# Seven-product gates: queries, keys and six gate columns in three rolling sets, the value pair gathered in PSUM banks, one weight sum made by adding transfers

## The chip, the cores and the metric

The kernel runs on one core of one Trainium2 chip. The metric is the device time of one execution in microseconds. Of the kernel before there are three timed runs and one profiled execution.

## The reference

One hybrid decoder layer on x (512 x 1024, float32): a pre-norm, one wide projection, three token mixers with gates, an output projection, a conv FFN and a final norm. The change lies in the projection and its first consumers.

```python
u = rmsnorm(x, ln1_g);  proj = u @ w_in            # 1024 -> 1152 q | 1152 k | 1152 v | 1024 pool |
                                                   #         1024 z | 1536 xbc | 16 dt | 3 x 1024 gates
q, k, v: 18 heads of 64 in 3 groups of 6 (dilations 1, 4, 16), each group banded causal attention
xbc = silu(causal_dwconv(xbc, conv_w, conv_b))     # 4 taps, 12 columns of 128
ga, gb, gc = sigmoid(gate_pre + b_gate)            # 8 columns of 128 each
m = ga * attn + gb * pool + gc * ssd;  x += m @ w_o;  x += conv_ffn(rmsnorm(x));  out = rmsnorm(x)
```

## The kernel before

**Matmuls in three terms.** float32 operands are split into a high part (float32r, cast on ScalarE) and a low part (the rest, subtracted on VectorE). A product is wh*xh + wh*xl + wl*xh, in this order (`mm3`, L234). A column of 128 outputs over 1024 inputs takes 24 matmuls of 512 columns.

**Jobs.** The work of TensorE is a list of `Job`s from `program()`. Each has weight sources, and before job n runs, a `prepare` step does three things for its successors: `low` (VectorE, L215) of the weights of job n+1, `cast` (ScalarE, L195) of those of n+2, and `fetch` (SyncE, L183) of those of n+3 into one of two `raw` tiles. The cast goes out in two halves through the list `second`: a half is emitted at each `step()`, or before the next job at the latest. A `job.form` gives a tile that is no fetched one, `job.then` is called behind the low part, and a `Call` runs a function at its place in the list.

**Steps.** `step()` first emits what is in `second`, then takes one more item from `waiting` (attention heads, scan chunks) and moves every running item on by one phase. An attention item (`attend`, L751 to L797) makes scores for two heads on TensorE, adds the bias and takes the maximum on VectorE, and makes four exponentials on ScalarE (L772); two steps later it turns them on TensorE.

**Queues.** The orders of TensorE, ScalarE, VectorE and GpSimd are the program's own. SyncE's transfers are ordered by the framework's scheduler.

**Quarter products.** For some products the 2 x 2 blocks of u and of the weights are multiplied in seven quarter products, with sums of u quarters (`sums_of_u`, `US`) and sums of weight quarters. Before, this is done for the value columns of groups 1 and 2 (`v_pair`, `sevens`: seven products into PSUM tiles `pb`, copied out and added on VectorE, L373 to L381 and L619) and for queries and keys of group 1 (`qk_sevens`: seven products of three columns, in banks). The eight gate columns of branch 1 are plain (`gate_jobs`, evacuated by a sigmoid and multiplied into the pool branch `MG`, L1166 to L1168), and so are the twelve columns of XBC (`xbc_evac`: one ScalarE pass, L911, and three convolution steps on VectorE, L915).

**Order of the stage:** pool branch; gates 0 to 3; the value pair; "one", "five", "two", "three" of queries/keys; gates 4 and 5; "six"; gates 6 and 7; "seven", "four"; `attend(1)`; XBC columns 0 to 11; the scan.

**Values.** The rows of the value columns are spread by sends from SBUF to SBUF, four for each 128 rows (`vr<-v`, L624), issued by SyncE.

Of the kernel before, what the change touches and what calls it, by code (L numbers as in the profile page):

```python
# [16 lines left out]
P = 128  # L17
# [66 lines left out]
def trunk(ctx: ExitStack, tc, out, x, rel_bias, ln1_g, w_in, b_gate, w_a, pool_w, pool_scale, w_b,  # L84
# [235 lines left out]
    def sums_of(f0, f1, ah, al, found):  # L320


        sa, sb = T("sa"), T("sb")
        dve.tensor_tensor(sa[:, LO], f0[:, HI], f1[:, HI], OP.add)
        dve.tensor_tensor(sa[:, HI], sa[:, LO], f0[:, LO], OP.subtract)
        dve.tensor_tensor(sb[:, LO], f0[:, LO], f0[:, HI], OP.subtract)
        dve.tensor_tensor(sb[:, HI], f1[:, LO], sa[:, HI], OP.subtract)
        yield
        bh, bl = T("sbh", F32R), T("sbl", F32R)
        act.copy(ah, sa)  # L330
        act.copy(bh, sb)
# [10 lines left out]
    def sevens(quarter, c, side, W, emit):  # L342

        r1, r2, r3, r5 = {}, {}, {}, {}

        def job(j, load, form, use):
            def body(ws):
                wh, wl = ws  # L350
                parts = side(j)
                for i in range(2):
                    ps = MM("pb")
                    o = slice(i * P, (i + 1) * P)
                    mm3(ps[:, :c], lambda k: wh[:, k, :], lambda k: wl[:, k, :],
                        lambda k: parts[k][0][:, o], lambda k: parts[k][1][:, o], range(4), flip=True)
                    use(i, ps[:, :c])
                step()
            new = Job([load] if load is not None else [], 4, c, body)
            new.form = form  # L360
            if load is None:
                new.load = lambda: None
            return new

        def keep(r, name):
            def use(i, ps):
                r[i] = T(name)[:, :c]
                act.copy(r[i], ps)
            return use

        def p5(i, ps):
            keep(r5, "r5")(i, ps)
            dve.tensor_tensor(r2[i], r2[i], ps, OP.add)  # L373

        def p6(i, ps):
            dve.tensor_tensor(r1[i], r1[i], ps, OP.add)
            emit(0, 1, i, r1[i], r2[i])

        def p7(i, ps):
            r3[i] = T("r3")[:, :c]  # L380
            dve.tensor_tensor(r3[i], r1[i], ps, OP.add)  # L381
            emit(1, 1, i, r3[i], r5[i])

        one = job("A11", quarter(0, 0), None, keep(r1, "r1"))
        two = job("A12", quarter(1, 0), None, lambda i, ps: emit(0, 0, i, r1[i], ps))
        three = job(4, None, lambda: W[1], keep(r2, "r2"))
        one.then = lambda: diff(one.raw, W[0], one.raw)
        three.then = lambda: diff(W[0], W[1], W[0])
        two.then = lambda: diff(W[1], W[1], one.raw)
        yield one  # L390
        yield three
        yield two
        yield job(1, None, lambda: one.raw, p5)
        yield job(2, None, lambda: W[1], p6)
        yield job(3, None, lambda: W[0], p7)
        yield job("A22", None, lambda: diff(two.raw, two.raw, W[1]),
                  lambda i, ps: emit(1, 0, i, r3[i], ps))
# [3 lines left out]
    def sums_of_u(p):  # L401

        f = []
        for k in (2 * p, 2 * p + 1):
# [4 lines left out]
                           lambda j, h, l: US.__setitem__((j, p), (h, l)))  # L409
# [195 lines left out]
    def v_pair():  # L605
# [3 lines left out]
        quarter = lambda two, h: rows_(c + 384 * h)[two]  # L609

        def load():
            for two in range(2):
                W.append(ypool.tile([P, 4, S], F32, name="w3", tag="xs")[:, :, :384])
                sp.dma_start(W[two], quarter(two, 1))

        def emit(hi, right, i, a, ps):
            g, tb = 1 + right, 2 * hi + i
            t = T(f"v{g}")
            dve.tensor_tensor(t[:, :384], a, ps, OP.add)  # L619

            for n in range(4):
                if (g, n) not in V:
                    V[g, n] = T(f"vr{g}")
                sp.dma_start(V[g, n][32 * tb:32 * tb + 32, :384], t[n:P:4, :384])  # L624

        return load, sevens(quarter, 384, side_u, W, emit)
# [20 lines left out]
    def qk_sevens(g):  # L647

        cols = (C_Q + 384 * g, C_K + 384 * g)
        q = lambda two, h: w_in[:, cols[h]:cols[h] + 384].rearrange(  # L650
            "(k two p) c -> two p k c", two=2, p=P)[two]
        W, X, Z, Y, r1, r5 = [], {}, {}, {}, {}, {}

        def load():
            for h in range(2):
                W.append(ypool.tile([P, 4, S], F32, name="w3", tag="xs")[:, :, :384])
                sp.dma_start(W[h], q(h, 1))

        def at(banks, c):
            return banks[c // 2][:, (c % 2) * 256:(c % 2) * 256 + 256]  # L660

        def half(which, c, hi):
            if (which, g, c) not in QK:
                QK[which, g, c] = T(f"{which}{g}")
            t = QK[which, g, c]
            t = grouped(t, g) if which == "q" else plain(t, g)
            return t[:, :, 64 * hi:64 * hi + 64]

        def turned_(ap):
            return ap.rearrange("p (j r) -> p r j", r=4)  # L670

        def job(source, j, banks, name, use, form=None):
            def body(ws):
                wh, wl = ws
                parts = side_u(j)
                for c in range(3):
                    fresh = name is not None
                    if fresh and c % 2 == 0:
                        banks[c // 2] = (MM if banks is Y else SM)(name)
                    cs = slice(c * P, (c + 1) * P)  # L680
                    mm3(at(banks, c), lambda k: wh[:, k, cs], lambda k: wl[:, k, cs],
                        lambda k: parts[k][0], lambda k: parts[k][1], range(4),
                        fresh and c % 2 == 0, True, again=not fresh or c % 2 == 1)
                    if c:
                        for done in (0, 1) if c == 1 else (2,):
                            use(done)
                        step()
            new = Job([source] if source is not None else [], 4, 384, body)
            new.form = form
            if source is None:  # L690
                new.load = lambda: None
            return new

        def keep(r, name, banks, scale):
            def use(c):
                r[c] = T(name)[:, :256]
                act.mul(r[c], at(banks, c), scale)
            return use

        def p2(c):  # L700
            dve.scalar_tensor_tensor(half("q", c, 0), turned_(at(Y, c)), 0.125, turned_(r1[c]),
                                     OP.mult, OP.add)

        def p6(c):
            r = T("r2")[:, :256]
            act.copy(r, at(X, c))
            dve.tensor_tensor(half("k", c, 0), turned_(at(Z, c)), turned_(r), OP.add)

        def p7(c):
            r = T("r7")[:, :256]  # L710
            act.copy(r, at(X, c))
            dve.tensor_tensor(half("k", c, 1), turned_(r), turned_(r5[c]), OP.add)

        def p4(c):
            act.mul(half("q", c, 1), turned_(at(X, c)), 0.125)

        one = job(q(0, 0), "A11", X, "p1", keep(r1, "r1", X, 0.125))
        one.then = lambda: diff(W[0], W[0], one.raw)
        two = job(q(1, 0), "A12", Y, "p2", p2)
        five = job(None, 1, Z, "p5", keep(r5, "r5", Z, 1.0), lambda: W[0])  # L720
        three = job(None, 4, Z, None, lambda c: None, lambda: W[1])
        three.then = lambda: diff(W[1], W[1], W[0])
        six = job(None, 2, X, None, p6, lambda: W[1])
        seven = job(q(0, 0), 3, X, None, p7, lambda: diff(seven.raw, W[1], seven.raw))
        four = job(q(1, 0), "A22", X, None, p4, lambda: diff(four.raw, four.raw, W[1]))
        return load, [one, five, two, three], [six, seven, four]

# [176 lines left out]
    def xbc_evac(m, ps):  # L904
        if m < 8:
            if m % 4 == 0:
# [253 lines left out]
    MG, MH, SG = {}, {}, {}  # L1160

# [314 lines left out]
    def program():  # L1476
# [11 lines left out]
        load, pair = v_pair()  # L1488
        yield Call(load)
# [266 lines left out]
```

## Time and profile before

| | us |
|---|---|
| timed runs | 1035.77, 1034.72, 1035.15; median 1035.15 |
| the profiled execution | 1034.7 |
| its span | 1033.0 |

| engine | busy us | share |
|---|---|---|
| TensorE (PE) | 1022.2 | 99% |
| weight loads (PEld) | 863.1 | 84% |
| VectorE (DVE) | 690.9 | 67% |
| ScalarE (ACT) | 473.3 | 46% |
| GpSimd (POOL) | 149.6 | 14% |

A row of the timeline or the chain begins with the start, counted in us from the span's start, and the length. A group of instructions names line, engine, operation, output and inputs, then shape and count; in brackets stand the idle time before it and what ended that. SPq is SyncE issuing transfers.

### The profile page before, as it was taken

Reading aid. Unit: us, or ns where it says so; the run is one execution under the profiler, and the core shown is the slowest. Engines: PE = TensorE matmul, PEld = TensorE weight load, DVE = VectorE, ACT = ScalarE, POOL = GpSimd, SP = SyncE. Lnnn points to the kernel's source line nnn. Section 1 sums busy time; section 2 is a strip of 40 time slices with the busy share of each in tenths; the row PEclk is TensorE's granted clock in tenths of the full one; section 3 lists DMA queues with packets and bytes.
Section 4 is the critical chain, followed back from the end, with each engine's and each line's share of the span. In section 5 each row is a group of like instructions: output and inputs, shape, how many; then the busy total and the mean of one; then the engine's idle time right before and its main releaser. Section 6 shows DMA issues by size and latency. Waiting matters only on the chain.

```text
span 1033.0 us, 13348 instructions
## 1 busy us (share of the span) xinstructions
PE 1022.2 (99%) x5312; PEld 863.1 (84%) x5312; DVE 690.9 (67%) x921; ACT 473.3 (46%) x779; POOL 149.6 (14%) x125
## 2 busy tenths in 40 slices
PE   9999999999999999999999999999999999999997
PEld 9998878899888878888888888898888888888885
DVE  5553566687567658766768656766768676666775
ACT  6432554453356364557445324545444443453342
POOL 2770000000000004210152501101111001111120
PEclk9999999999999999999999999999999999999999
DMA  8344312035242244452244525543233324323142
GB/s 289 115 129 138 109 54 75 31 102 172 94 139 84 86 127 116 144 140 67 67 148 152 174 82 204 171 141 121 82 102 124 102 82 163 123 81 122 62 143 82
DMA packets 115997, 122.35 MB, mean 118 GB/s; under 512 B 5315, under 2 KB 98310, under 8 KB 115935
## 3 DMA queue, kind: packets, MB, share of 16 engines
q1 hardware_dynamic: 115343, 120.64, 36.7%
q8 instruction: 42, 0.69, 0.3%
q10 hardware_dynamic: 592, 0.86, 0.3%
q14 instruction: 20, 0.16, 0.1%
HBM read 117.69 MB, written 2.22 MB: 116 GB/s over the span
## 4 chain that ended last, share of the span: by engine, by line
PE 93%; DVE 3%; ACT 2%; DMA 1%; issue 1%; ACTq 0%; SPq 0%; DVEq 0%
PE pa L234 35%; PE pu L234 21%; PE pb L234 10%; PE p L234 10%; PE pqk L234 6%; PE pa L1607 2%; PE ps L751 1%; PE pu L1407 1%; DVE wl L215 1%; PE ppw L234 1%; PE pt L779 1%; PE po L792 1%; PE py L1077 1%; ACT wh L195 1%; DMA xin<-in_x_dram 1%; PE pyo L1084 1%
## 5 line engine op out<-in xcount | busy, mean ns | idle before, releaser
L215 DVE TENSOR_TENSOR wl<-raw,wh 128x2048 fp32r<-128x2048 f32 (+3 forms) x96 | 218.5, 2278 | 46.7 <-ACT wh L195 38.8
L195 ACT CAST wh<-raw 128x1024 fp32r<-128x1024 f32 (+3 forms) x190 | 189.9, 1017 | 54.9 <-DVE raw L339 32.3
L1268 DVE SCALAR_TENSOR_TENSOR hc<-pu,fcol,hc 128x510 f32<-128x510 f32 x88 | 65.8, 748 | 61.0 <-ACT hc L1265 59.4
L234 PE MATMUL pa<-uh,wh 128*128 128x512 f32 x384 | 98.6, 399 | 0.0
L234 PE MATMUL pa<-ul,wh 128*128 128x512 f32 x384 | 94.9, 389 | 0.0
L234 PE MATMUL pa<-uh,wl 128*128 128x512 f32 x384 | 94.9, 389 | 0.0
L234 PEld LDWEIGHTS pa<-ul,wh 128*128 128x128 f32 x384 | 72.1, 188 | 15.2
L234 PEld LDWEIGHTS pa<-uh,wl 128*128 128x128 f32 x384 | 72.1, 188 | 14.9
L234 PE MATMUL pu<-uh,wl 128*128 128x512 f32 (+1 forms) x352 | 83.6, 380 | 0.2 <-DVE wl L215 0.2
L234 PE MATMUL pu<-uh,wh 128*128 128x512 f32 (+1 forms) x352 | 83.6, 379 | 0.0
L234 PE MATMUL pu<-ul,wh 128*128 128x512 f32 (+1 forms) x352 | 83.5, 379 | 0.0
L234 PEld LDWEIGHTS pa<-uh,wh 128*128 128x128 f32 x384 | 70.1, 188 | 14.5 <-issue 0.7
L234 PEld LDWEIGHTS pu<-uh,wl 128*128 128x128 f32 x352 | 64.1, 188 | 13.0 <-DVE wl L215 0.6
L234 PEld LDWEIGHTS pu<-ul,wh 128*128 128x128 f32 x352 | 64.2, 188 | 12.5
L234 PEld LDWEIGHTS pu<-uh,wh 128*128 128x128 f32 x352 | 64.1, 188 | 12.4
L1273 POOL TENSOR_TENSOR hc<-hc 128x512 f32<-128x512 f32 x22 | 30.4, 1383 | 279.2 <-DVE hc L1268 244.2
L1265 ACT ACTIVATE hc<-pu,fcol,fcol 128x512 f32<-128x512 f32 x40 | 31.2, 780 | 82.0 <-PE pu L234 81.7
L1039 POOL TENSOR_TENSOR xd<-xc,dec 128x512 f32<-128x512 f32 x6 | 6.4, 1063 | 331.5 <-DVE xc L1033 312.6
L772 ACT ACTIVATE sb<-sb,both 128x128 f32<-128x128 f32 (+1 forms) x72 | 30.1, 419 | 33.2 <-DVE both L769 23.2
L1166 ACT ACTIVATE sg<-pa,col 128x512 f32<-128x512 f32 x24 | 16.5, 688 | 58.1 <-PE pa L234 51.3
L1270 ACT ACTIVATE hc<-hc 128x512 f32<-128x512 f32 x22 | 13.9, 632 | 42.9 <-DVE hc L1268 42.9
L915 DVE SCALAR_TENSOR_TENSOR xs<-pa,col,xs 128x509 f32<-128x509 f32 (+2 forms) x24 | 18.0, 749 | 16.4 <-ACT xs L911 15.8
(377 smaller groups left out, 1863.1 us busy)
## 6 DMA issues: line engine op xcount, KB each, us to landing
raw<-in_w_in_dram SPq DMA_DIRECT2D x25, 1024.0 KB
raw<-in_ffn_w_up_dram SPq DMA_DIRECT2D x22, 1024.0 KB
raw<-in_ffn_w_down_dram SPq DMA_DIRECT2D x11, 1024.0 KB
raw<-in_w_o_dram SPq DMA_DIRECT2D x8, 1024.0 KB
raw<-in_w_in_dram SPq DMA_DIRECT2D x14, 512.0 KB
raw<-in_w_in_dram SPq DMA_DIRECT2D x8, 768.0 KB
raw<-in_w_b_dram SPq DMA_DIRECT2D x4, 1024.0 KB
al<-ad SPq DMA_DIRECT2D x16, 256.0 KB
```

The costliest lines, as they stand in the source:

```text
L195: act.copy(job.high[:, :, o], job.raw[:, :, o])
L215: (eng or dve).tensor_tensor(l[:, :, o], job.raw[:, :, o], h[:, :, o].bitcast(F32), OP.subtract)
L234: pe.matmul(ps, l, r, start=first and n == 0, stop=last and n == total - 1, skip_group_check=again)
L751: pe.matmul(pss[i][:, o:o + w * P], q[r, n * P:(n + 1) * P], k[r, kb * P:(kb + w) * P], start=True, stop=True)
L772: act.activation(sb[:, off:off + w * P], sb[:, off:off + w * P], AF.Exp, bias=nm[:, n, h:h + 1], accum_out=ls[:, n, h:h + 1])
L915: dve.scalar_tensor_tensor(t[:, sh:], ps[:, :S - sh], col[:, o_cw + 12 * k + m:o_cw + 12 * k + m + 1], t[:, sh:], OP.mult, OP.add)
L1166: act.activation(s, ps, AF.Sigmoid, bias=col[:, o:o + 1])
L1265: act.activation(t, ps, AF.Identity, bias=ff["c1"][:, ff["b"] + m:ff["b"] + m + 1], scale=fw(2, m))
L1268: dve.scalar_tensor_tensor(t[:, sh:], ps[:, :S - sh], fw(k, m), t[:, sh:], OP.mult, OP.add)
L1270: act.activation(t, t, AF.Silu)
L1273: pool.tensor_tensor(a, a, t, OP.mult)
L1607: pe.matmul(first[2 * n + j][:, lo:hi], a[:, k, j * P:(j + 1) * P], b[:, k, lo:hi], start=a is wh and b is uh and k == 0, stop=a is wl and ...
```

## The change

1. **Sets.** `qk_sevens` goes. `set_of_sevens` makes seven quarter products for two left and two right columns of 128 at a time, each product 24 matmuls of 256 columns into one bank. Three sets: queries 0, 1 with keys 0, 1; query 2 and gate 0 with key 2 and gate 1; gates 2, 3 with gates 4, 5. The sets roll: products of the next stand between those of the last. Four PSUM banks ("c", "y", "a", "b") are held through all three. `step()` runs after every second product.
2. **Weight sums.** Product "one" reads W[0], the set's own load. W[0] += W[1] serves "five", then += the raw tile of "three" for "six", then += that of "two" for "four". For "seven" W[1] gets the fourth quarter added by transfers that GpSimd issues (`accum_op`). One sum of u changes its sign.
3. **Value pair.** Order one, five, two, three, six, seven, four; products gather in banks X (one, six, seven, four) and Z (five, three).
4. **Gates.** `gate_sink`: left gates add the copy of "one" and take a sigmoid for the low half at "two", and a sigmoid straight from the bank at "four"; right gates subtract at "six" and "seven" and take one sigmoid over both halves. Each ends in the multiplication into `MG`.
5. **Places.** XBC columns 8, 9 and gates 6, 7 stand ahead of the pair; XBC columns 10 and 11 are single-column jobs ahead of "seven" and "four" of the third set; `attend(1)` is called after "four" of the second set; then XBC columns 0 to 7.

The core of the diff:

```diff
-    def sevens(quarter, c, side, W, emit):
...
+    def sevens(quarter, c, W, body):
+        jobs = {}
+        def plus(to, what):
+            dve.tensor_tensor(to, to, what, OP.add)
+        def put(name, source=None, w=0):
+            job = jobs[name] = Job(source or [], 4, c,
+                                   lambda ws: body(name, ws, side_u(SIDES[name])))
+            if source is None:
+                job.load = lambda: None
+                job.form = lambda: W[w]
+        for name in ("one", "five", "six", "four"):
+            put(name)
+        put("seven", w=1)
+        put("two", quarter(1, 0))
+        put("three", quarter(1, 1))
+        def first_sum():
+            plus(W[0], W[1])
+            at = 0
+            for src in quarter(1, 1):
+                n = src.shape[-1]
+                for k in (0, 2):
+                    pool.dma_start(W[1][:, k:k + 2, at:at + n], src[:, k:k + 2, :], accum_op=OP.add)
+                at += n
+        jobs["one"].then = first_sum
+        jobs["three"].then = lambda: plus(W[0], jobs["three"].raw)
+        jobs["six"].then = lambda: plus(W[0], jobs["two"].raw)
+        return jobs
...
+    def set_of_sevens(lefts, rights, x, scales=(1.0, 1.0)):
...
+        def body(name, ws, parts):
+            wh, wl = ws
+            ps = bank(role.get(name, x))
+            fresh = name in ("one", "two", "five")
+            for c in range(2):
+                cs = slice(c * P, (c + 1) * P)
+                mm3(cut(ps, c), lambda k: wh[:, k, cs], lambda k: wl[:, k, cs],
+                    lambda k: parts[k][0], lambda k: parts[k][1], range(4),
+                    fresh and c == 0, True, again=not fresh or c == 1)
+            use(name, ps)
+            turn_of[0] += 1
+            if turn_of[0] % 2 == 0:
+                step()
...
+    def gate_sink(b, m, left):
+        t = T("gr")
+        def gate(to, ps):
+            o = o_bg + 8 * b + m
+            act.activation(to, ps, AF.Sigmoid, bias=col[:, o:o + 1])
+        def times():
+            dve.tensor_tensor(MG[m], MG[m], t, OP.mult)
+        def two(ps, r):
+            dve.tensor_tensor(t[:, LO], ps, r, OP.add)
+            gate(t[:, LO], t[:, LO])
+        def four(ps):
+            gate(t[:, HI], ps)
+            times()
+        def put(hi, x, y):
+            dve.tensor_tensor(t[:, (LO, HI)[hi]], x, y, OP.subtract)
+            if hi:
+                gate(t, t)
+                times()
+        return (two, four) if left else put
...
         yield Call(load)
-        yield from gate_jobs(1, 0, SPLIT)
-        load, begun, ended = qk_sevens(1)
+        yield from BC(8, 10, 256)
+        yield from gate_jobs(1, 6, 8)
         for i, job in enumerate(pair):
             yield job
-            if i == 5:
-                yield Call(load)
-        yield from begun
-        yield from gate_jobs(1, SPLIT, SPLIT + 2)
-        yield ended[0]
-        yield from gate_jobs(1, SPLIT + 2)
-        yield from ended[1:]
-        yield Call(lambda: attend(1))
-        yield from jobs_a(w_in, C_XBC, 12, uhk, ulk, KD, xbc_evac)
+            if i in (4, 5):
+                yield Call(loads[i - 4])
+        spare = BC(10, 12, P)
+        for i, n in ((0, "one"), (0, "five"), (0, "two"), (0, "three"), (0, "six"), (1, "one"),
+                     (0, "seven"), (1, "five"), (0, "four"), (1, "three"), (1, "two"), (1, "six"),
+                     (2, "one"), (1, "seven"), (2, "five"), (1, "four"), (2, "three"), (2, "two"),
+                     (2, "six"), (2, "seven"), (2, "four")):
+            if (i, n) == (0, "four"):
+                yield Call(loads[2])
+            if (i, n) in ((2, "seven"), (2, "four")):
+                yield next(spare)
+            yield s[i][n]
+            if (i, n) == (1, "four"):
+                yield Call(lambda: attend(1))
+        yield from BC(0, 8, 256)
```

Here `BC(lo, hi, width)` makes jobs of the XBC columns lo to hi - 1.

More of the change, by code (lines that the diff above doesn't have):

```diff
@@ L340, in diff @@
         return out
-    def sevens(quarter, c, side, W, emit):
[L346 to L397, printed above, removed]
@@ new lines, in trunk @@
+    SIDES = {"one": "A11", "two": "A12", "three": 4, "four": "A22", "five": 1, "six": 2, "seven": 3}
+    def sevens(quarter, c, W, body):
[25 more added lines that the diff above has]
+        return jobs
@@ L609, in v_pair @@
         quarter = lambda two, h: rows_(c + 384 * h)[two]
+        X, Y, Z, r1, r5 = {}, {}, {}, {}, {}
+        banks = {"one": X, "six": X, "seven": X, "four": X, "five": Z, "three": Z, "two": Y}
         def load():
[L612 to L616, printed above, removed]
+            for h in (1, 0):
+                W.insert(0, ypool.tile([P, 4, S], F32, name="w3", tag="xs")[:, :, :384])
+            for h in range(2):
+                sp.dma_start(W[h], quarter(0, h))
@@ L628, in qk_jobs @@
+        jobs = sevens(lambda two, h: [quarter(two, h)], 384, W, body)
+        return load, [jobs[n] for n in ("one", "five", "two", "three", "six", "seven", "four")]
     def qk_jobs(g):
@@ L654, in load @@
         def load():
+            w = ypool.tile([P, 4, S], F32, name="w3", tag="xs")
             for h in range(2):
[L656 to L726, printed above, removed]
+                W.append(w[:, :, 256 * h:256 * h + 256])
+                for j, src in enumerate(quarter(0, h)):
+                    sp.dma_start(W[h][:, :, src[0]:src[1]], src[2])
```

140 lines of the change are left out of this document (124 added, 16 removed).

## The prediction

> **What bounds the kernel now.** I read the page's busy times and its chain first, then the waits of TensorE, the busy times of single stages, and last the timeline around the lines that the diff touches.
>
> ```profile
> PE 1022.2 (99%) x5312; PEld 863.1 (84%) x5312; DVE 690.9 (67%) x921; ACT 473.3 (46%) x779; POOL 149.6 (14%) x125
> PE 93%; DVE 3%; ACT 2%; DMA 1%; issue 1%; ACTq 0%; SPq 0%; DVEq 0%
> PE p L234 <- DVE wl L215: 0.5, 1, 0.5
> 188.00:364.00 176.00, 175.54 (x1034) 154.73 (x1029) 121.74 (x132) 79.37 (x150) 0.00 (x0) 1.00 0.32 102
> 190.00:206.00 16.00, 16.00 (x72) 13.18 (x72) 12.87 (x21) 5.63 (x10) 0.00 (x0) 1.00 0.00 1
> 206.00:241.20 35.20, 34.77 (x214) 34.52 (x212) 29.43 (x29) 16.42 (x27) 0.00 (x0) 1.00 0.38 122
> ```
>
> TensorE is the bound: 99% busy, 93% of the chain. The fourth row (window and length, then PE, PEld, DVE, ACT, POOL, clock, DMA) is the stretch that the change rewrites, 188 to 364 us: TensorE lacks 0.46 us there, which is the one wait of the third row, in the query/key products; the clock is full. VectorE is busy 12.9 of 16 us ahead of the value pair and 29.4 of 35.2 us in it. So the change can win only by fewer matmul columns, and loses wherever a weight split comes later than TensorE.
>
> **Matmuls.** Six gate columns become quarter products: 6 x 24 = 144 matmuls of 512 columns go, and 21 products of 24 matmuls of 256 (504) replace 252 such for queries and keys. The pair (168 of 384) and the twelve XBC columns keep their counts; two XBC columns and two gates stand elsewhere.
>
> ```profile
> 253.48 10.91 PE pa L234 x48
> 279.61 8.63 PE p L234 x72
> ```
>
> A 512-column matmul takes 10.91/48 = 0.2273 us, one of 256 8.63/72 = 0.1199, slightly over half. So -144 x 0.2273 = -32.7 and +252 x 0.1199 = +30.2: **-2.5 us**. The one wait of 0.5 us is in code that goes: **-0.5**. No more can be won.
>
> **The value pair** gathers in PSUM banks, which takes VectorE additions away and adds none to TensorE: 0. It was hidden under TensorE before, so it pays nothing either.
>
> **Start of the first set.** Before, product "one" read a fetched tile; now it reads W[0], the set's own load. In the order of the built program SyncE has, during the pair: the fetch for the set's "two" (which needs the pair's raw tile, free only after W[0] += raw behind "six"), eight sends of the pair's "two", the fetch for "three", W[0], four sends, W[1], twelve sends, and only then the second set's load.
>
> ```profile
> 206.19 0.87 PE L234 MATMUL pb<-wh,uh 128*128 128x384 f32 x4
> 235.34 0.63 PE L234 MATMUL p<-uh,wh 128*128 128x256 f32 x4
> 235.31 0.53 SPq L183 DMA_DIRECT2D raw<-in_w_in_dram  x1
> 235.94 10.54 SPq L624 DMA_DIRECT2D vr<-v  x16
> 240.12 0.83 ACT L195 CAST wh<-raw 128x768 fp32r<-128x768 f32 x1 [0.18 <-DMA raw<-in_w_in_dram]
> 202.26 0.62 ACT L330 CAST sah<-sa 128x512 fp32r<-128x512 f32 x1
> 202.79 0.62 ACT L331 CAST sbh<-sb 128x512 fp32r<-128x512 f32 x1
> 234.29 1.75 DVE L215 TENSOR_TENSOR wl<-raw,wh 128x1536 fp32r<-128x1536 f32 x1
> 290.22 2.29 DVE L215 TENSOR_TENSOR wl<-raw,wh 128x2048 fp32r<-128x2048 f32 x1 [2.56 <-ACT wh L195]
> ```
>
> The pair takes 29.15 us, 4.16 a product, so the first set should start at 235.3. When is the raw tile free? "five" ends at 214.5; then come, each on the one before, copy and cast of "three" (2.1), its low part and the addition into W[0] (2 x 1.7), the cast of "six" (1.6), its low part and the addition of the tile (3.3): 224.9. A send costs SyncE 10.54/16 = 0.66 us, a fetch 0.53: + 0.5 + 8 x 0.66 + 0.5 gives W[0] its issue at 231.2. 768 KB took 4.8 us from issue to the cast that had waited for it; the fetch for "three" and W[0] are 1 MB together, so W[0] lands at about 236. Two half casts (one every 0.53, together 1.1) and the low part (2.29/2, say 1.2) put wl at 238.3, where TensorE, eight matmuls in, wants it at 236.3: 2.0. "five" needs W[1], four sends later, the addition, cast and low part: about 1.0 more. Sum **+3.0** (1.9 to 4.5: 0.66 against 0.76 a send, and the landing). Behind the waiting cast stand the pair's last copies on ScalarE, and nobody needs these soon.
>
> **Inside the sets.** A product takes 24 x 0.12 = 2.88 us; its weight must be cast and subtracted in about 3.84 us after the job two before it ends, for wl is wanted eight matmuls in.
>
> ```profile
> 190.13 0.59 ACT L797 COPY o<-po 128x512 f32<-128x512 f32 x1
> 200.95 0.69 ACT L1166 ACTIVATE sg<-pa,col 128x512 f32<-128x512 f32 x1 [2.99 <-PE pa L234]
> 269.97 1.14 DVE L707 TENSOR_TENSOR k<-p,r 128x256 f32<-128x256 f32 x2
> ```
>
> Copy 0.59, two half casts 1.1, low part 1.2: 2.9 us, so a plain product is in time. With a gate on the right side, "seven" of the second set puts two subtractions (1.14) and a sigmoid (0.69) ahead of the next cast in ScalarE's queue: 4.6 us, 0.8 late. The same with "two" and "six" of that set: 0.1 and 0.6. **+1.5**, bounds 0 and 3; the second set's own load, behind the twelve sends, may add **0.5**.
>
> **Third set, spare XBC columns and attention.** The attention of group 1 now starts during the third set, one item at each step. A step emits, in this order on ScalarE: first half of a cast, the item's four exponentials, second half. Before, the same items ran beside XBC jobs of 10.9 us:
>
> ```profile
> 293.64 1.16 PE L751 MATMUL ps<-k,q 64*128 64x128 f32 x16
> 293.75 0.78 ACT L911 ACTIVATE xs<-pa,col 128x512 f32<-128x512 f32 x1 [3.56 <-PE pa L234]
> 294.43 1.04 ACT L195 CAST wh<-raw 128x1024 fp32r<-128x1024 f32 x1
> 294.56 2.31 DVE L915 SCALAR_TENSOR_TENSOR xs<-pa,col,xs 128x509 f32<-128x509 f32 x3 [2.04 <-ACT xs L911]
> 295.48 1.28 ACT L772 ACT_TABLE_LOAD   x1
> 296.79 0.68 DVE L765 TENSOR_TENSOR sb<-ps,b 128x512 f32<-128x512 f32 x1
> 297.51 0.69 DVE L769 TENSOR_REDUCE both<-sb 128x4 f32<-128x512 f32 x1
> 298.23 0.40 ACT L772 ACTIVATE sb<-sb,both 128x128 f32<-128x128 f32 x1 [1.47 <-DVE both L769]
> 299.69 0.19 ACT L772 ACTIVATION_READ_ACCUMULATOR sb<-sb,both 128x1 f32 x1
> 319.99 0.65 PE L779 MATMUL pt<-eye,sb 128*128 128x128 f32 x4
> 202.98 0.68 DVE L1168 TENSOR_TENSOR yo<-yo,sg 128x512 f32<-128x512 f32 x1
> ```
>
> The exponentials start 4.6 us after an XBC column ends, because VectorE does the convolution first, and they end 6.2 us after it. With 10.9 us jobs nobody noticed. Now one product of 2.88 us lies between. I walk ScalarE's queue.
>
> (1) From the end of "two": two additions 1.1, two short sigmoids to 1.55, half cast to 2.15, table load to 3.45, exponentials (ready at 2.6) to 5.1, second half to 5.7. TensorE does scores 1.1 and "six" 2.9, and wants column 10 at 4.0. The single column reads both halves at once: **1.7 late**.
> (2) From the end of column 10: second half after 6.2 + 0.6 = 6.9. TensorE does "seven" 2.9, scores and a turn (1.1 + 0.6), wants column 11 at 4.6: **2.3 late**.
> (3) From there ScalarE and VectorE alternate for the two gates of "seven": copy to 7.4, sigmoid table to 8.65, then subtraction, sigmoid, multiplication twice, to 11.7; scores' addition and reduction to 13.05; four exponentials to 14.75, second half to 15.3, low part of "four" 16.5. TensorE finishes column 11 (5.45) at 12.3, turns 0.6, eight matmuls: 13.85: **2.7 late**; "four" ends at 18.45.
> (4) Column 11's evacuation to 16.0, half cast of columns 0/1 (1.04), convolution on VectorE to 18.75, bias and reduction to 20.05, exponentials to 21.75, copy, second half to 23.25, low part (2.29) 25.6; TensorE wants it after 16 matmuls, at 22.1: **3.5 late**.
>
> Sum **+10.2**. Queued behind the exponentials are the half cast for TensorE's next job and, behind that, every later evacuation. Afterwards each job has 10.9 us again. The columns 8 and 9 that move ahead of the pair take 3 convolution steps (2.31) in place of one gate multiplication (0.68) each on VectorE: 3.3 us more where it was busy 12.9 of 16; the additions that the pair's "five" needs end 1.7 later, near 205, and its cast is due at 207, so 0, and up to 1.7 if that cover is gone. Bounds: 7, if each hand-over is 0.8 quicker than the rows; 14, with slower table changes:
>
> ```profile
> 365.59 1.28 ACT L1096 ACT_TABLE_LOAD   x1
> 366.88 1.16 ACT L1096 ACTIVATE xcv<-xcv 128x512 f32<-128x512 f32 x2
> ```
>
> Here the next activation starts 1.29 us after the load began, and I reckon with that. The Trainium skill (page "ScalarE: Activation LUTs", section "What ACT_TABLE_LOAD costs") gives 1.28 us for the load and about 1.38 us of drain besides, for every change of set; this trace has no such drain in these rows. By that section the three loads in (1) and (3) would cost an estimated 3 x 1.38 = 4.1 us more, and the sum would be so much higher.
>
> **Adding transfers.** GpSimd issues them and has nothing else in this stretch (POOL 0.00 in the three windows at the top). The trace has none. A load of 768 KB took 4.8 us; the sum in W[1] is wanted some 13 us after its issue in the first set (addition at 239.5, cast of "seven" at 253), 17 or more elsewhere. Below zero they cannot go, since nothing on the path is removed by them; at three times the plain load's time they are still just covered. I take 0. The Trainium skill ("DMA: Bandwidth & Descriptors", section "Anatomy of one DMA — SWDGE (gpsimd) path") fits 2.0 us + bytes/436e3 for such queues, from which I estimate 3.2 us for 512 KB, with 0 as well.
>
> **Sum.** -2.5 - 0.5 + 3.0 + 1.5 + 0.5 + 10.2 = +12.2 on the profiled execution's 1034.7 us (span 1033.0), which is 0.45 under the median 1035.15: **1047.3 us** in the median. Lower ends: -3.0 + 1.9 + 0 + 0 + 7 = +5.9, 1041; upper ends: -3.0 + 4.5 + 3 + 1.5 + 14 = +20, of which all at once is unlikely; I close at +18.5, 1053.5.
>
> **Rivals.**
> *The matmul count wins.* Place: the second half casts and low parts from "two" of the third set on. If ScalarE's exponentials ran before TensorE's products were through (in (1) 1.7 us sooner, in (4) 3.5), and W[0] landed 2 us earlier, only -2.5 - 0.5 is left: 1032.2. For it: TensorE is 99% busy and the count is sure. Against it: the exponentials' 6.2 us are in the rows. 6%.
> *Only the start costs.* If the walks (1) to (4) overlap better than a queue in order allows, by half or more, -3.0 + 3.0 + 0.5 and some 3 us: 1036 to 1041. 10%.
> *Adding transfers late.* If the 512 KB of a sum took over 13 us, ScalarE's cast of the first set's "seven" waits, behind it the scaled copies of the second set and every later cast. At 20 us: +7 on top, 1054; from 13 us on it decides. Nothing in the trace speaks for such a slow transfer. 10%.
> That the products are not what the change says cannot be: the built order has the 504 matmuls.
>
> **Chances.** Forecast 72% (its own range 1041 to 1053.5), the others 6, 10 and 10%, no change 2%. 0.2% or 2.1 us is what a measurement here can tell. Faster 0.06, same 0.02, slower 0.92. The range 1041 to 1053.5 leaves out the two low cases and most of the late transfers.
>
> **What would show it.** In the profile after: 5420 PE instructions; a PE wait list with column 10 and 11 (pa) behind ScalarE's wh, 1.7 and 2.3 us, "four" behind wl, 2.7, columns 0/1 behind wl, 3.5; the first set's "one" and "five" behind W's landing, 3 us; some 14 us less than full PE between 235 and 330; four more table loads; no PE wait on a "seven" for DMA. Wrong if these waits sum to under 6 us, if the 256-column matmuls take other than 0.12 us, or if the stretch before 235 or after 330 moves.

## The result: 9.7 us slower, and where the time is lost

The changed kernel takes 1045.04 us in the median of four runs (1044.45 to 1045.56), the kernel before, run beside it, 1035.3 (1034.72 to 1035.77): a ratio of 1.0094 with a 95% interval of 1.0077 to 1.0112. Forecast were 1047.3 and 1041.0 to 1053.5.

First the page of the changed kernel: engines, the clock in 40 slices, the transfers of GpSimd's queue, and the chain by engine.

```profile
span 1043.1 us, 13694 instructions
PE 1025.3 (98%) x5420; PEld 870.1 (83%) x5420; DVE 699.1 (67%) x938; ACT 490.1 (47%) x815; POOL 161.7 (15%) x135
PEclk9999999999998999999999999999999999999999
q0 software_dynamic: 2720, 2.36, 1.7%
PE 93%; ACT 3%; DVE 2%; DMA 1%; issue 0%; ACTq 0%; DVEq 0%
```

TensorE has 108 matmuls more, as counted (252 - 144), and still 93% of the chain. VectorE's share fell from 3 to 2% and ScalarE's rose from 2 to 3. One of the 40 slices of the clock shows an 8, where all slices of the kernel before show a 9 (90% or more).

The waits of TensorE that bear on this (line, what it waited for, us in total, times, longest), and four of them in its timeline:

```profile
PE pa L234 <- ACT wh L195: 3.5, 2, 2.2
PE p L234 <- DVE wl L215: 3.3, 2, 2.7
...
PE pcb L1056 <- ACT xcv L1144: 1.0, 1, 1.0
...
PE pa L234 <- DVE wl L215: 0.4, 1, 0.4
...
295.65 2.11 PE L234 MATMUL pa<-uh,wh 128*128 128x512 f32 x8 [1.27 <-ACT wh L195]
308.12 2.12 PE L234 MATMUL pa<-uh,wh 128*128 128x512 f32 x8 [2.18 <-ACT wh L195]
317.97 1.22 PE L234 MATMUL p<-uh,wl 128*128 128x256 f32 x4 [2.70 <-DVE wl L215]
318.99 1.05 PE L234 MATMUL p<-uh,wh 128*128 128x256 f32 x4
321.55 3.18 PE L234 MATMUL pa<-uh,wh 128*128 128x512 f32 x8
324.57 1.99 PE L234 MATMUL pa<-ul,wh 128*128 128x512 f32 x8
326.94 2.10 PE L234 MATMUL pa<-uh,wl 128*128 128x512 f32 x8 [0.39 <-DVE wl L215]
```

These are column 10, column 11, "four" and columns 0/1, in the places of walks (1) to (4): 1.27, 2.18, 2.70 and 0.39 us. (The 3.3 of the list holds one more wait, of 0.56 us at 282.29; the wait of `pcb`, a product of the scan, 1.0 us, stands in the kernel before as well.) Between the last two waits of the timeline, eight matmuls of 512 columns take 3.18 us in the row at 321.55, where as many take 1.99 in the row at 324.57. The stage by windows (length, then PE, PEld, DVE, ACT, POOL, granted clock, DMA share, GB/s) says why:

```profile
317.25:324.07 6.82, 6.10 (x22) 5.57 (x23) 4.11 (x6) 3.59 (x12) 0.00 (x0) 0.50 0.00 0
```

The granted clock was 0.50 for 6.82 us, and it fell while TensorE stood in the wait of 2.70 us. Sixteen matmuls of 256 columns, from 317.97 to 321.55, took 3.58 us where 16 x 0.1199 = 1.92 were due, and the next eight of 512 took 3.02 instead of 1.82: 2.9 us.

The span grew by 10.1 us. Of this 0.84 lies ahead of the pair, whose first product starts at 207.03 instead of 206.19; the kernel with extra matmuls below, the same up to there, starts it at 206.16, and in all kernels below, whose edits act on what comes later, this start lies between 205.75 and 207.01, so this part is not put down to the change. The other 9.3 are: -2.5 and -0.5 of the forecast, 6.5 of the four waits, 1.45 of four gaps of 0.2 to 0.7 us inside the sets, 2.9 of half clock, and a rest of 1.4 in gaps under 0.2 us between products.

### The profile page after: what moved, and what is told of

Read it like the earlier page. It is cut to its first block, busy times and chain, and to the rows that moved or that the text cites. A ratio compares the mean times of both kernels' runs of the same rounds, so it can differ in the third digit from the quotient of the medians.

```text
span 1043.1 us, 13694 instructions
## 1 busy us (share of the span) xinstructions
PE 1025.3 (98%) x5420; PEld 870.1 (83%) x5420; DVE 699.1 (67%) x938; ACT 490.1 (47%) x815; POOL 161.7 (15%) x135
## 4 chain that ended last, share of the span: by engine, by line
PE 93%; ACT 3%; DVE 2%; DMA 1%; issue 0%; ACTq 0%; DVEq 0%
PE pa L234 31%; PE pu L234 22%; PE p L234 15%; PE pb L234 8%; PE pqk L234 6%; PE pa L1696 2%; PE pu L1481 1%; PE ppw L234 1%; PE ps L799 1%; PE po L840 1%; PE pt L827 1%; PE py L1125 1%; DVE wl L215 1%; ACT sb L820 1%; DMA xin<-in_x_dram 1%; ACT wh L195 1%
## 5 line engine op out<-in xcount | busy, mean ns | idle before, releaser
L215 DVE TENSOR_TENSOR wl<-raw,wh 128x2048 fp32r<-128x2048 f32 (+3 forms) x94 | 208.8, 2223 | 57.3 <-ACT wh L195 50.1
L195 ACT CAST wh<-raw 128x1024 fp32r<-128x1024 f32 (+3 forms) x186 | 180.8, 994 | 44.5 <-DVE raw L339 26.4
L234 PE MATMUL pa<-uh,wh 128*128 128x512 f32 x336 | 87.8, 404 | 3.5 <-ACT wh L195 3.5
L234 PE MATMUL pa<-uh,wl 128*128 128x512 f32 x336 | 83.1, 389 | 0.4 <-DVE wl L215 0.4
L234 PE MATMUL pa<-ul,wh 128*128 128x512 f32 x336 | 83.1, 389 | 0.0
L234 PEld LDWEIGHTS pa<-uh,wl 128*128 128x128 f32 x336 | 63.0, 188 | 13.8 <-DVE wl L215 0.8
L234 PEld LDWEIGHTS pa<-ul,wh 128*128 128x128 f32 x336 | 63.1, 188 | 13.3
L215 DVE TENSOR_TENSOR wl<-w,wh 128x1024 fp32r<-128x1024 f32 (+2 forms) x25 | 38.5, 1541 | 10.6 <-ACT wh L195 10.6
L370 POOL DMA_DIRECT2D w<-in_w_in_dram x10 | 12.3, 1230 | 194.4 <-DVE w L349 164.8
L195 ACT CAST wh<-w 128x512 fp32r<-128x512 f32 (+2 forms) x50 | 35.2, 746 | 15.0 <-DVE w L349 9.7
```

Of the source, the lines that this page charges most:

```text
L195: act.copy(job.high[:, :, o], job.raw[:, :, o])
L215: (eng or dve).tensor_tensor(l[:, :, o], job.raw[:, :, o], h[:, :, o].bitcast(F32), OP.subtract)
L234: pe.matmul(ps, l, r, start=first and n == 0, stop=last and n == total - 1, skip_group_check=again)
L370: pool.dma_start(W[1][:, k:k + 2, at:at + n], src[:, k:k + 2, :], accum_op=OP.add)
```

## The experiments

Each was timed beside the kernel before on one chip; a ratio is against that.

### Attention put in line after the third set

```diff
-            if (i, n) == (1, "four"):
+            if (i, n) == (2, "four"):
                 yield Call(lambda: attend(1))
```

> One call moved: the attention of group 1 is put in line when the third set's product "four" has been done instead of the second set's, so its items run beside the later XBC columns (products of 10.9 us) and no longer beside the set's 2.88 us products. Theory (the exponentials stand in ScalarE's queue between the two halves of a cast, and only short products suffer): the four waits of the changed kernel, 1.27 (column 10), 2.18 (column 11), 2.70 ("four") and 0.39 us (columns 0/1), go, and with them the 2.9 us of half clock; 1045.0 - 9.4 = 1035.6 us, and up to 1.1 less if the small gaps between jobs go too (1034.5). Rival 1 (the two XBC columns within the set cause it by their convolution on VectorE, attention or not): the waits for columns 10 and 11 stay, 1041 to 1045. Rival 2 (the later start of attention moves its own end behind the work that needs it): waits of another name near 364 to 376 us, time between 1036 and 1040.

1033.56 us, ratio 0.9981 (0.9971 to 0.9990): 0.9 under the lowest time that the theory gave. The waits of TensorE in this kernel, whole list of those over 0.1 us:

```profile
PE pa L1653 <- DVE relb L502: 1.1, 1, 1.1
PE p L234 <- DVE wl L215: 0.8, 2, 0.6
PE pxs L1079 <- DVE o L845: 0.2, 1, 0.2
PE po L840 <- ACT sb L828: 0.2, 1, 0.2
```

Both waits for columns 10 and 11 are gone, though the columns stand where they stood; nothing new came later, and no slice of the clock is below 9. One moved call is worth 11 us. A wait of 1.0 us further on is gone too, which the kernel before and the changed kernel both have; in the kernel before it is

```profile
370.69 1.16 PE L1008 MATMUL pcb<-xcv 128*128 128x128 f32 x8 [0.98 <-ACT xcv L1096]
```

From the pair's start to the end, this kernel takes 1031.9 - 206.60 = 825.3 us against 1033.0 - 206.19 = 826.8 before: 1.5 less, and 1.0 of it is that wait. The sets by themselves thus gain some 0.5 us only. The forecast's terms without the four walks and without a start give -2.5 - 0.5 + 1.5 = -1.5; they leave out the gaps under 0.2 us (1.4 in the changed kernel).

### Both halves of a cast ahead of the exponentials

```diff
+    TOGETHER = [False]
...
     def step():
         flush()
+        while TOGETHER[0] and second:
+            flush()
...
             if (i, n) == (1, "four"):
                 yield Call(lambda: attend(1))
+                yield Call(lambda: TOGETHER.__setitem__(0, True))
         yield from BC(0, 8, 256)
+        yield Call(lambda: TOGETHER.__setitem__(0, False))
```

> While the third set and the first attention items run, a step emits both halves of a cast ahead of the item's exponentials; before, the second half stood behind them. Nothing is left out, and attention stays where the change put it. Theory (what is paid is the place of the second half in ScalarE's queue): the waits for columns 10 and 11 (1.27 and 2.18 us) go, the one for "four" is 2.7 to 3.4 and the one for columns 0/1 0.4 to 1.3; half clock stays only if a wait over about 2.5 us is left: 1039.8 us, 1038 to 1042. Rival (ScalarE is simply too full between 292 and 324 us, in whatever order): the waits move behind the next jobs and the sum stays, 1044 to 1046.

1039.34 us, ratio 1.0036 (1.0022 to 1.0050), as the theory had it. The waits in its timeline from 300 us on:

```profile
310.17 0.74 PE L238 MATMUL p<-uh,wh 128*128 128x256 f32 x4 [0.62 <-ACT wh L199]
313.44 0.74 PE L238 MATMUL p<-uh,wl 128*128 128x256 f32 x4 [2.06 <-DVE wl L219]
320.19 2.11 PE L238 MATMUL pa<-uh,wl 128*128 128x512 f32 x8 [0.92 <-DVE wl L219]
338.22 1.09 PE L844 MATMUL po<-sb,vr 128*64 128x128 f32 x14 [1.64 <-ACT sb L832]
```

Columns 10 and 11 no longer wait, "four" waits 0.62 + 2.06, columns 0/1 0.92: the order of a cast's second half and the exponentials was what made the columns late. But 1.64 us come back in the attention, which waits for its own exponentials. These waits sum to 5.2 us; the clock stays full. (The wait of `pcb` is absent here too, and in the next two runs.)

### The gates moved too: first the sigmoids, then the multiplications

```diff
+        def later(f):
+            second.append(lambda: second.append(f))
...
-                gate(t, t)
-                times()
+                def rest():
+                    gate(t, t)
+                    times()
+                later(rest)
```

and so for the other places of a gate.

> Attention stays where the change put it. Both halves of a cast ahead of an item's exponentials, and the gates' sigmoids and multiplications also behind both halves. Theory (ScalarE and VectorE have room enough between 292 and 330 us; only the place in their queues makes weights late): "four"'s wait of 2.06 us in the version with both halves ahead, which stood behind two gates and a table load, falls under 0.8; what exponentials come later costs at most 1.6 us at the attention's own products: 1036.5 us (1035.5 to 1038). Rival (too full in whatever order): the sum of the waits between 290 and 345 us stays near 5.2 us, 1039 or more.

1039.04 us, ratio 1.0033 (1.0020 to 1.0046): the theory failed. "Four" waited 2.77 us, the attention 1.88, and the clock fell 1.4 us after the first of them had ended. VectorE's timeline and one window of the stage show it:

```profile
305.23 0.76 DVE L1238 TENSOR_TENSOR gr<-five,r 128x256 f32<-128x256 f32 x2 [1.07 <-ACT r L735]
308.30 1.31 DVE L1222 TENSOR_TENSOR yo<-yo,gr 128x512 f32<-128x512 f32 x2 [2.31 <-ACT gr L1219]
309.52 0.69 DVE L817 TENSOR_TENSOR sb<-ps,b 128x512 f32<-128x512 f32 x1
...
311.44 1.22 DVE L219 TENSOR_TENSOR wl<-w,wh 128x1024 fp32r<-128x1024 f32 x1
...
313.00:318.00 5.00, 5.00 (x24) 4.43 (x24) 4.59 (x6) 3.17 (x8) 0.00 (x0) 0.66 0.00 0
```

In the window's 5 us the granted clock was 0.66 on average. The halves were cast by 306.2, but their low part stood behind two multiplications that waited 2.31 us for the sigmoids, and behind an addition, a reduction and a copy. So the next run put the multiplications (`times`) behind the next low part, at the head of the next step:

```diff
     def step():
+        while after_low:
+            after_low.pop(0)()
         flush()
...
-                    times()
+                    after_low.append(times)
```

> As the version with both halves and the deferred gates (1039.0 us, waits of 2.77 us on "four" and 1.88 us in the attention), but the gates' multiplications on VectorE are put behind the next product's low part; the sigmoids stay where they were. In that version ScalarE had "four"'s halves done at 306.2, and VectorE began their low part only at 311.44: it waited 2.31 us for the sigmoids' result, then did two multiplications, addition, reduction and a copy first. Theory (what is late is decided by which operation stands ahead in an engine's queue, VectorE's here): the low part comes at about 309.7, the wait is about 1.0 us, the clock stays full and the 1.7 us that half clock took go too: 1035.6 us (1035 to 1037). Rival (ScalarE and VectorE are too full between 292 and 330 us in whatever order): the 1.8 us turn up in another wait before 345 us: 1038.5 or more.

1037.42 us, ratio 1.0021 (1.0011 to 1.0031). Its waits:

```profile
312.94 2.12 PE L240 MATMUL pa<-uh,wh 128*128 128x512 f32 x8 [1.63 <-ACT wh L201]
319.07 2.11 PE L240 MATMUL pa<-uh,wl 128*128 128x512 f32 x8 [2.19 <-DVE wl L221]
336.80 1.09 PE L846 MATMUL po<-sb,vr 128*64 128x128 f32 x14 [1.33 <-ACT sb L834]
```

"Four" doesn't wait at all now, but columns 0/1 wait 1.63 + 2.19 and the attention 1.33: 5.15 us, against 5.2 in the first order and 2.77 + 1.88 = 4.65, with half clock besides, in the second. The expected 1.0 us on "four" and 1035.6 us were not met, and the rival, that the time turns up in another wait, holds. What this run gained on the first order, 1.9 us, came within the sets: from the pair's start to column 10 it takes 292.37 - 206.63 = 85.74 us, the first order 293.47 - 205.75 = 87.72 (moving the gates is worth 1.8 us in the last experiment). So the order in the queues explains the way from 9.4 us (waits and half clock) down to about 5. Those 5 stayed in all three orders: from column 10's start to the second `pcb` product of the scan they take 88.65, 89.00 and 88.28 us, and 83.73 with attention later.

### Matmuls in place of the idle wait

```diff
+    def keep_warm():
+        ps = MM("pwarm")
+        for i in range(12):
+            pe.matmul(ps, uh[:, 0, :P], uh[:, 0, :], start=True, stop=True)
...
+            if (i, n) == (2, "four"):
+                yield Call(keep_warm)
```

> Twelve matmuls of 512 columns, whose result nobody reads, stand ahead of the third set's "four", in the place where TensorE waited 2.70 us; 12 x 0.227 = 2.7 us. All other work is as in the changed kernel. Theory (the half clock of 317.25 to 324.07 us comes from the idle 2.70 us, and what it costs would else have been the fourth wait, since ScalarE's exponentials make columns 0/1 that late anyway): clock 1.0 throughout, the wait for columns 0/1 grows from 0.39 to about 3.3 us, time as the changed kernel within 0.4 us. Rival (the half clock costs on its own account): the 2.9 us go, 1042.1 us. If the clock falls all the same, an idle wait isn't its cause.

1044.97 us, ratio 1.0092 (1.0077 to 1.0107): the time of the changed kernel.

```profile
313.25 3.02 PE L1553 MATMUL pwarm<-uh 128*128 128x512 f32 x12
326.15 3.62 PE L234 MATMUL pa<-uh,wl 128*128 128x512 f32 x8 [3.15 <-DVE wl L215]
...
326.00:328.00 2.00, 1.85 (x4) 1.50 (x5) 1.47 (x4) 1.80 (x2) 0.00 (x0) 0.51 0.31 58
328.00:330.00 2.00, 2.00 (x9) 1.29 (x9) 2.00 (x1) 0.18 (x1) 0.00 (x0) 0.64 1.06 369
```

The wait for "four" is filled, and that for columns 0/1 is 3.15 us instead of 0.39. From column 10's start to the low part of columns 0/1 the two kernels take the same: 326.94 - 295.65 = 31.29 and 326.15 - 294.86 = 31.29 us. So the end of this stretch is set by ScalarE and VectorE, and the 2.9 us of half clock lay inside what would have been the fourth wait. The expectation that the clock would stay full failed: it fell in the wait of 3.15 us instead, and there it had a price. The eight matmuls behind that wait take 3.62 us, against 2.10 in the changed kernel. Its profiled span is 0.8 us longer, although its pair started 0.87 us sooner; that the medians agree within 0.1 us is thus partly chance.

### Two table loads less

```diff
-                gate(t, t)
+                gate(t, t, AF.Exp if SHORT[0] else AF.Sigmoid)
```

`SHORT` is set from the third set's "seven" on. The kernel leaves out the sigmoid of two gates, whose factor comes out otherwise.

> The changed kernel, with the exponential in place of the sigmoid in the two gates of the third set's "seven" (that factor of the gates comes out otherwise), so that two table loads of 1.28 us, at 308.6 and 312.9 us, fall away on ScalarE. Theory (the chain of waits: only the first stands on the chain, the second lies beside VectorE's addition and reduction, which end at 314.47, and no load has a drain behind it): "four"'s wait 2.70 becomes 1.4, columns 0/1's weights come 1.3 us sooner, and the half clock doesn't come since no wait is over 2.2 us: 1043.7 us (1043.2 to 1044.2). Rival 1 (both loads count): 1042.4. Rival 2 (each load has a drain of about 1.38 us besides, as a rule of the notes has it): 1041.1 or, with one load on the chain, 1042.4 with a gap behind the load in the rows of the changed kernel, which doesn't show one.

1045.67 us, ratio 1.0095 (1.0081 to 1.0109): all theories wrong. ScalarE in the changed kernel, then in this one (its stretch lies 1.03 us earlier, by column 10's start):

```profile
308.58 1.28 ACT L1215 ACT_TABLE_LOAD   x1
309.87 0.72 ACT L1215 ACTIVATE gr<-gr,col 128x512 f32<-128x512 f32 x1
```

```profile
308.66 0.73 ACT L1217 ACTIVATE gr<-gr,col 128x512 f32<-128x512 f32 x1 [1.14 <-DVE gr L1231]
316.76 0.74 PE L234 MATMUL p<-uh,wl 128*128 128x256 f32 x4 [2.53 <-DVE wl L215]
325.73 3.69 PE L234 MATMUL pa<-uh,wl 128*128 128x512 f32 x8 [3.14 <-DVE wl L215]
```

Without the load the sigmoid's place waits 1.14 us for VectorE's subtraction, so both loads lay beside VectorE's work and cost 0.17 us together (2.70 - 2.53). After the wait of 2.53 us the clock stayed full, but what was taken off came back at columns 0/1, whose low part again set the end: TensorE goes on with it 31.11 us after column 10's start, against 31.29. The half clock then came behind the wait of 3.14 us and made eight matmuls 3.69 us long.

### The adding transfers replaced by an addition

```diff
-                    pool.dma_start(W[1][:, k:k + 2, at:at + n], src[:, k:k + 2, :], accum_op=OP.add)
...
-        jobs["three"].then = lambda: plus(W[0], jobs["three"].raw)
+        jobs["three"].then = lambda: [plus(w, jobs["three"].raw) for w in W]
```

> The four adding transfers of each set are left out, and the same sum W[1] + raw of "three" is done by VectorE with one addition of 128x2048 (128x1536 in the value pair) behind "three". Theory (the adding transfers are hidden and cost nothing): the same time within 0.5 us, VectorE busy some 4 x 2.3 us more, no new TensorE wait over 1 us; a bit slower, up to +1.5 us, if the additional addition in the third set comes ahead of the convolution. Rival (their 512 to 768 KB or GpSimd's use of VectorE's port hold other transfers or VectorE up): faster by 1 us or more, with the wait for "four" shorter.

1047.49 us, ratio 1.0117 (1.0102 to 1.0132): against the changed kernel's ratio 0.0023 or 2.4 us more, over what either theory gave. Two of its waits, absent in the changed kernel, in the first set:

```profile
240.51 0.74 PE L234 MATMUL p<-sah,wl 128*128 128x256 f32 x4 [0.57 <-DVE wl L215]
250.15 0.74 PE L234 MATMUL p<-sah,wl 128*128 128x256 f32 x4 [0.75 <-DVE wl L215]
```

The transfers are worth their place: the additions on VectorE delay low parts. From the pair's start to column 10 this kernel takes 297.12 - 206.12 = 91.0 us, the changed one 88.6. Then columns 0/1 wait 1.85 us instead of 0.39, and a second stretch of half clock follows. That the transfers themselves cost nothing is not isolated by this run; no wait of TensorE in the changed kernel names one. (The trace has ten of them: two for the pair; two, four and two for the sets.)

### The first set's load issued later

On the kernel with the later attention, five of the value pair's sends are issued twice:

```diff
                 send()
+                if (name, i) == ("two", 1):
+                    for n in (0, 1, 2, 3, 0):
+                        sp.dma_start(V[1, n][32:64, :384], t[n:P:4, :384])
```

> On the version with attention put in line later (1033.6 us, no wait over 0.6 us in the sets): SyncE issues five of the value pair's sends twice, same data to the same rows, between the send of "two" and the fetch of "three". 5 x 0.63 = 3.2 us, so the first set's W[0] is issued near 231.1 instead of 227.9 us, which is where the prediction had put it. Theory (the +3.0 us term for the start was wrong only in that time of issue): W[0]'s casts end near 237.8, its low part near 239.1 where TensorE wants it at 237.2; a wait of 1.6 to 2.0 us on "one", up to 1 more on "five": 1035.2 to 1036.6 us. Rival (the landing or the casts have more slack than the rows say): under 0.6 us, 1033.6 to 1034.2.

1044.41 us, ratio 1.0085 (1.0071 to 1.0098), for a reason that neither theory had. SyncE's queue, then two waits of TensorE, "five" and "three":

```profile
221.04 0.37 SPq L183 DMA_DIRECT2D raw<-in_w_in_dram  x1
221.51 5.02 SPq L606 DMA_DIRECT2D vr<-v  x8
226.63 3.09 SPq L632 DMA_DIRECT2D vr<-v  x5
229.82 0.53 SPq L714 DMA_DIRECT2D w<-in_w_in_dram  x1
...
249.62 0.58 SPq L183 DMA_DIRECT2D raw<-in_w_in_dram  x1
...
241.11 0.74 PE L234 MATMUL p<-sah,wl 128*128 128x256 f32 x4 [0.57 <-DVE wl L215]
254.12 1.22 PE L234 MATMUL p<-sbh,wh 128*128 128x256 f32 x4 [7.95 <-ACT wh L195]
```

The framework's scheduler, which orders SyncE's transfers, put the fetch for "three" behind the sends, at 249.62 instead of 226.2, and "three" waited 7.95 us. As a test of the start it still says something: W[0] went out 2.3 us later than in its base (229.82 against 227.49), and "one" did not wait. "Five", whose sum needs the later W[1], did, 0.57 us, as the prediction's second part of the start would have it. The issue time of 231.2 that the prediction had was not reached.

### Both cures: the later attention and the deferred gates

The two diffs together (attention after the third set; sigmoids and multiplications of all gates behind both halves of a cast).

> Attention put in line after the third set (1033.6 us) and, in all three sets, the gates' sigmoids and multiplications put behind both halves of a cast. Theory (the waits left within the sets, 0.57, 0.27 and five or six of 0.2 us, come from additions, subtractions and a sigmoid that stand ahead of a product's second half): about 1 us of them goes, 1032.7 us (1032.3 to 1033.2). Rival (they come from the copy out of PSUM and the low part, which stay): 1033.6 within 0.3.

1031.72 us, ratio 0.9961 (0.9948 to 0.9973): the fastest, 4.1 us under the kernel before. One wait over 0.2 us is left between 200 and 420 us:

```profile
280.79 0.74 PE L234 MATMUL p<-uh,wl 128*128 128x256 f32 x4 [0.48 <-DVE wl L215]
```

From the pair's start on its span is 1030.1 - 206.64 against 1033.0 - 206.19 before: 3.4 us less. Of this 1.0 is the wait of `pcb`, so 2.4 are left for the sets, where fewer matmul columns and the old wait were put at 3.0 and 0.48 us are still waited. The forecast for this run, 1032.7, was 1.0 too high.

## Why the prediction was right, point by point

- **Matmul count, -2.5, and old wait, -0.5: right.** The last kernel shows 2.4 of the 3.0 us, with a wait of 0.48 left.
- **Value pair, 0: right.** Its seven products still follow one another without a wait, 29.15 us in both kernels.
- **Start of the first set, +3.0: wrong, 0 was measured.** The step that failed is the time of issue. The prediction had SyncE's fetch for the set's "two" wait for the raw tile that the pair's "two" frees behind "six". It took the one of the pair's "three":

```profile
219.23 1.75 DVE L349 TENSOR_TENSOR w<-w,raw 128x1536 f32<-128x1536 f32 x1
221.06 0.37 SPq L183 DMA_DIRECT2D raw<-in_w_in_dram  x1
227.92 0.37 SPq L711 DMA_DIRECT2D w<-in_w_in_dram  x1
233.47 1.14 ACT L195 CAST wh<-w 128x512 fp32r<-128x512 f32 x2 [0.77 <-DMA w<-in_w_in_dram]
```

  The addition that frees it ends at 220.98, 3.9 us ahead of the 224.9 that the prediction had, so W[0] was issued at 227.92 instead of 231.2. The tile that is free behind "six", at 226.23, took the fetch for "three" (226.64). The casts of W[0] began at 233.47, ended at 234.6, and TensorE wanted them at 236.2. Its low part ended at 235.87 and was wanted at 237.12, 1.25 us later; 3.3 us more would give an estimated wait of 2.0, which is the prediction's own figure for "one", but no run issued W[0] so late.
- **Inside the sets, +1.5 (+0.5 for the second set's load): place and size right,** 1.45: 0.95 at the second set's "four", behind its "seven", for 0.8, and 0.21 and 0.28 for 0.1 and 0.6. Not in the prediction are the gaps under 0.2 us, 1.4 together. The second set's load held nothing up: its 0.5 was not measured.
- **Third set, +10.2: right in place, order and sum.** (1) 1.27 for 1.7, (2) 2.18 for 2.3, (3) 2.70 for 2.7, and (4) 0.39 with 2.9 of half clock, or 3.15 with TensorE kept busy, for 3.5: 9.4 in all. Shown by moving the attention: without it all four are gone. Not right was a reason in (3): the walk puts the subtraction behind the sigmoid's table load, but the load lies beside VectorE's low part and subtraction, which end only 0.2 us before it (309.66 and 309.86). Without both loads the wait is 2.53 us. That the time of (3) still came out to the tenth is luck in this step. The Trainium skill (page "ScalarE: Activation LUTs", section "What ACT_TABLE_LOAD costs") adds 1.38 us of drain to each change; here the load of 308.58 ends at 309.86 and the sigmoid starts at 309.87. This trace shows no drain there.
- **Adding transfers, 0: right,** and better than the addition in their place.
- **The sum, 1047.3 for 1045.04: partly luck.** Of +12.2 us, 3.0 for the start, 0.5 for the second set's load and 0.8 in the walks were too much. Gaps under 0.2 us, which the prediction had not, gave 1.4 back, and the profiled execution started 0.84 late: +10.1. So errors of two signs left a difference of only 2.3 us.
- **The signs.** 5420 matmuls, 0.12 us for one of 256 columns, four more table loads (32 for 28) and no wait on a "seven" for a transfer were met. The four waits sum to 6.5 us, little over the 6 that would have spoken against it. Between 235 and 330 us 7.3 are idle and 2.9 lost by half clock, 10 for the 14 forecast. Half clock itself was not in the prediction.

What exactly holds the last 5 us in the three orders with early attention stays open. They moved from product to product with their sum kept; no run separated ScalarE's share from VectorE's.

## What to carry to other kernels

When the products between two hand-overs get shorter, look first at what else runs beside them: a chain that hid beside 10.9 us products (here scores, maximum, four exponentials, 4.6 to 6.2 us) cost 9.4 us here beside products of 2.88 us, and moving its start was worth more than any order within it. Before a wait is priced, ask which engine's queue sets the end of the stretch: filling the wait and removing two table loads left the time where it was within the noise, and half clock cost nothing where it took up the time of a later wait, but 1.5 us where it came behind the last one. And where a tile pool decides when a transfer can go, find in the order of releases which tile it gets.

## What the hardware showed beyond that

The granted clock fell to 0.5 in or just behind waits of TensorE of 2.70 us (the changed kernel), 2.71, 2.77, 3.15, 3.14 and 7.95 us (in the runs above), and did not with waits of 2.53, 2.19, 2.18 and 2.06 us; in the run without adding transfers it fell again behind one of 1.85 us. So the length of a wait does not decide by itself. Nor does the place: the fall came 2.0 us into the wait of 2.70, and 1.4 us after the end of that of 2.77.

What does repeat is the length of the half clock. In the changed kernel it was 6.82 us. Read in windows of 0.1 us, it lasted 3.4 us behind the waits of 2.77, 3.15 and 3.14 us and 10.2 around the end of that of 7.95. Without adding transfers it went from 318.9 to 322.3 and from 329.1 to 332.5, two stretches of 3.4 us whose starts lie 10.2 apart. All are near whole multiples of 3.4 us. The Trainium skill (page "TensorE: Matmul & The Clock Gate", section "Part 1: The HAM clock gate (the "warmup" mystery)") tells of free-running windows of about 3.4 us, an idle one of which halves the clock; the lengths here agree with such windows, but all waits except the one of 7.95 us are shorter than one. How much of a window must be idle, no run here settles. Counted back in steps of 3.4 from the fall at 325.8 in the run with two table loads less, the wait of 2.53 us (314.23 to 316.76) would be cut into two parts of some 1.3 and 1.2 us. That might be why it was without consequence; it is an estimate, and no run varied it.
